# A pre-norm layer with RWKV-7, neighbourhood attention and a mixture of experts on one core: one recurrence direction in reversed time, one block transpose per solve, head-by-head turns, and background matmuls handed out at a fixed rate

## The chip, the cores and the metric

The kernel runs on one core of a Trainium2 chip. The metric is the device time of one execution in microseconds (us), median over runs. Everything is computed in float32 or with pairs of fp32r matmuls that together give float32 accuracy.

## The reference, cut to what matters

One layer. The 256 latent tokens `x` and 256 context tokens `ctx` are modulated, normalised and projected by one large matrix. Two mixers read the projections: RWKV-7, a linear recurrence run in both directions over time, and neighbourhood attention. Their outputs are gated, merged, projected and added to `x`; then 16 experts, two per token, follow.

```python
def rwkv_scan(s0, r, decay, k, v, kk, a, reverse, emit):
    def step(s, inp):
        w_t, k_t, v_t, kk_t, a_t = inp[:5]
        s_kk = jnp.einsum('bhvk,bhk->bhv', s, kk_t)
        s = (s * w_t[:, :, None, :] - s_kk[..., None] * (kk_t * a_t)[:, :, None, :]
             + v_t[..., None] * k_t[:, :, None, :])
        y = jnp.einsum('bhvk,bhk->bhv', s, inp[5]) if emit else None
        return s, y
...
    for d in range(2):
        rev = d == 1
        s_c, yc_d = rwkv_scan(s0, r_c, w_c, kd_c, v_c, kk_c, a_c, rev, emit_ctx)
        _, yx_d = rwkv_scan(s_c, r_x, w_x, kd_x, v_x, kk_x, a_x, rev, True)
        y_x = y_x + yx_d
...
        yb_c, yb_x = na_mixer(z_c, z_x, na_q_g[l], na_k_g[l], na_rpb[l], need_ctx=not last)
        x = x + m_x[2] * branch_merge(z_x[9], z_x[10], ya_x, yb_x, proj_a[l], proj_b[l], w_out[l])
        h2_x = modulate(rms_norm(x, norm2_g[l]), m_x[3], m_x[4])
        x = x + m_x[5] * moe(h2_x, router_w, router_bias, moe_w1[l], moe_w3[l], moe_w2[l])
```

There are 8 heads of 64 channels in the recurrence and two directions, `d = 0` forward and `d = 1` backward.

## The kernel before, in words

The recurrence is cut into chunks of 32 tokens, 8 chunks per stream. It goes first over the context (`s = 0`), then over the latents (`s = 1`), and each of the two passes has three stages that follow one another:

- **prep** (`rw_prep`, L639): decays and keys on VectorE, ScalarE and GpSimd; `products` (L691) multiplies keys by keys within each chunk, on TensorE, one matmul for each chunk and half of the partitions, in blocks of 64 rows by 64 columns with 32 columns of the moving operand; `turn` (L720) transposes the scaled keys `bk` into `BT` (four 128x128 transposes at L727 for each `q`, then four copies of 64x256 out of PSUM at L731).
- **solve** (`rw_solve`, L757): the inverses of all unit triangular 32x32 matrices at once, on VectorE. It transposes the input in 32x32 blocks at L765 (four instructions, one for each 32 partitions; the two of direction 1 write through a reversed-dimension view), runs 31 dependent pairs at L770 and L772, and transposes back at L776 (four instructions). While it runs, `fill()` is called after every second pair.
- **chain** (`rw_chain`, L779): 8 dependent steps, one for each chunk. A step has small matmuls (32x32, 128x32 and 64x64 tiles), an eviction at L801, another at L809, the state update at L822 and, for the latents, the output products.

These three stages are called the recurrence's own work below. The rest of the layer up to the merge, called the other work, is a Python generator `others()` (L1041): values, attention projections and attention for two head groups, receptances, modulation, gates. Its matmuls are 128x128 tiles with 256 or 512 moving columns; every projection is three fp32r products of split operands (`three`, L431). `step()` (L477) advances the generator by at most three matmuls, and `fill()` (L472) at some 160 places of the recurrence's code takes the next number from the hand-written list `FILL` (L160) and makes so many steps. `until(name)` (L1060) steps until a named part is issued. Which instruction then stands where on an engine is decided by the scheduler of the tile layer, with the order of issue as the priority.

A weight unit is split into a high and a low part by ScalarE (L260) and VectorE (L261) when the generator first needs it (`w_unit`, L419). Outputs of 128x256 take one PSUM bank each (`proj_fm` L437, `proj_tm` L450), and each is evicted by its own instruction.

After the recurrence come the output gate, `proj_a`, the merge, the output projection `wo`, the router, and the 16 experts in 8 rounds of two, whose weights come by DMA.

```python
    def fill():
        for _ in range(next(fills, 0)):
            step()
...
        yield from values()
        done.add("v")
        yield from att_proj(0)
        yield from both_(att_core(0), att_proj(1), MIX[0])
        yield from receptances()
```

Of the kernel before, what the change touches and what calls it, by code (L numbers as in the profile page):

```python
# [63 lines left out]
def _constants():  # L64
# [52 lines left out]
def _pack(I):  # L117
# [42 lines left out]
FILL = [  # L160
# [4 lines left out]
]  # L165
ORDER = [(("k0", 1), ("k1", 0))] * 3
MIX = [7, 1]
# [60 lines left out]
def hybrid_kernel(ctx: ExitStack, tc: tile.TileContext, a, out, dbg=None, stop=None):  # L228
# [84 lines left out]
    def turn_x(st, k2):  # L313
        p = pb()
        for k in range(2):
            for i in range(2):
                kc = 2 * k2 + k
                T.transpose(p[:, (2 * k + i) * 128:(2 * k + i + 1) * 128], xn[:, 2 * st + i, kc * 128:(kc + 1) * 128], ident)
        (V.tensor_copy if k2 % 2 else S.copy)(xT[:, 2 * k2:2 * k2 + 2, st * 256:st * 256 + 256], p.rearrange("p (k t) -> p k t", k=2))
# [51 lines left out]
    def w_load():  # L371
        i = n_loaded[0]
        if i < len(SEQ):
# [37 lines left out]
    def w_raw(*name):  # L411
        i = n_used[0]
        n_used[0] += 1
        assert SEQ[i] == name, (SEQ[i], name)
        return wraw[i % NRAW]

    n_split = [0]

    def w_unit(*name):  # L419
# [5 lines left out]
        w_load()  # L425
        v = lambda t: t.r[:, :4 * w].rearrange("p (k c) -> p k c", c=w)
        return v(hi), v(lo)
# [9 lines left out]
    def proj_fm(n, nt):  # L437

        w = GROUPS[n][1]
        res = [pa()[:, :nt] for _ in range(w // 128)]  # L440
        for hf in range(2):
# [4 lines left out]
            yield from three([(res[c], at(wh, k, c), x[k], hf == 0 and k == 0 and x is hs, False) for c, k in ck for x in (hs, us)]  # L446
                             + [(res[c], at(wl, k, c), hs[k], False, hf == 1 and k == 3) for c, k in ck])
        return res

    def proj_tm(n):  # L450

        res = [pa()[:, :256] for _ in range(4)]
        for hf in range(2):
# [3 lines left out]
            yield from three([(res[tt], at(x, tt, k), wh[:, k, :], hf == 0 and k == 0 and x is hh, False) for tt, k in tk for x in (hh, hl)]  # L457
                             + [(res[tt], at(hh, tt, k), wl[:, k, :], False, hf == 1 and k == 3) for tt, k in tk])
        return res
# [9 lines left out]

    fills = iter(FILL)  # L470

    def fill():  # L472

        for _ in range(next(fills, 0)):
            step()

    def step():  # L477
        if filler[0] is not None and next(filler[0], "end") == "end":
            filler[0] = None
# [10 lines left out]
    def first_split(n, q):  # L490
# [8 lines left out]
        if q % 2:  # L499
            w_load()  # L500
# [95 lines left out]
    def mod_gen(m, rows):  # L596
        p = pb()
        for kc in range(8):
            b = w_raw("mod", m, kc)
            mod_part(p, kc, [b[:, 256 * g:256 * g + 256] for g in range(4)])  # L600
            w_load()
# [37 lines left out]
    def rw_prep(s, R):  # L639
# [21 lines left out]
        def decays(f, d):  # L661
# [18 lines left out]
            for h in range(2):  # L680
                r_ = slice(64 * h, 64 * h + 64)
                eng = G if h else V
                eng.tensor_tensor(GG[f][d][r_, h, :, :, 0, :], qc(kk[s][r_, Qs]), E4[r_, :, :, ex], op=ALU.mult)
                if s:
                    eng.tensor_tensor(GG[f][d][r_, h, :, :, 1, :], qc(R["rf"][r_, Qs]), E4[r_, :, :, inc], op=ALU.mult)
            V.scalar_tensor_tensor(bk[:, :, d, :], c16(sg), 0.5, c16(cum), op0=ALU.mult, op1=ALU.mult)
# [33 lines left out]
        def turn(f, d):  # L720
            bk = tmps[d][3]
            for q in range(2):
# [34 lines left out]
    def rw_solve(AT, nA, Xi, tmp):  # L757
# [5 lines left out]
        quarters = [(slice(32 * i, 32 * i + 32), i % 2) for i in range(4)]  # L763
        for ro, d in quarters:
            V.transpose(nA[ro].rearrange("p j s -> p s j") if d else nA[ro], ATg[ro])  # L765
# [9 lines left out]
        for ro, d in quarters:  # L775
            V.transpose(ATg[ro], Xi[ro].rearrange("p j s -> p s j") if d else Xi[ro])  # L776
# [68 lines left out]
    def values():  # L845
        for f in range(2):
            Qs = slice(2 * f, 2 * f + 2)
            for t4, p in enumerate((yield from proj_tm(f"v{f}"))):
                s, tt = divmod(t4, 2)
                S.copy((RC, RX)[s]["vt"][:, :, tt, Qs, :].rearrange("p h q v -> p q h v"), p.rearrange("p (q h v) -> p q h v", h=2, v=64))  # L850
# [13 lines left out]
    def att_proj(g):  # L864
# [6 lines left out]
        qs = yield from proj_fm(f"qB{g}", 256)  # L871
# [5 lines left out]
        for q, p in enumerate(qs):  # L877
            V.tensor_scalar(qB[:, q, :], p, W["qg"], None, op0=ALU.mult)
            S.activation(qsq[:, q, :], p, AF.Square)
        yield  # L880
        vs = yield from proj_tm(f"vB{g}")
        for tt, p in enumerate(vs):
            S.copy(vB[:, tt, :], p)
# [14 lines left out]
    def receptances():  # L898
        RX["rf"] = A.get(4, 256)
        for f in range(2):  # L900
            for q, p in enumerate((yield from proj_fm(f"r{f}", 256))):
                S.copy(RX["rf"][:, 2 * f + q, :], p)
# [8 lines left out]
    def gates_a():  # L911
        ga_alloc()

        (p,) = yield from proj_fm("lg", 256)
# [566 lines left out]
```

## Time and profile before

| what | value |
|---|---|
| median of three runs | 769.55 us (769.16, 769.55, 773.76) |
| the profiled execution's own time | 774.38 us |
| its span, first to last instruction | 772.6 us |
| TensorE (PE) busy, share of the span | 699.7 us, 91% |
| VectorE (DVE) busy | 415.7 us, 54% |
| ScalarE (ACT) busy | 301.4 us, 39% |
| mean granted TensorE clock | 0.919 of full |
| stages by their first own instruction | prep 0 from 72 us, solve 0 from 129, chain 0 from 176, prep 1 from 264, solve 1 from 350, chain 1 from 398, merge and `wo` from 484, experts from 539 |

All times of the rows are us from the start of the span. The time outside the span is 774.38 − 772.6 = 1.8 us.

### The profile page before, as it was taken

Reading aid. Unit: us, or ns where it says so; the run is one execution under the profiler, and the core shown is the slowest. Engines: PE = TensorE matmul, PEld = TensorE weight load, DVE = VectorE, ACT = ScalarE, POOL = GpSimd, SP = SyncE. Lnnn points to the kernel's source line nnn. Section 1 sums busy time; section 2 is a strip of 40 time slices with the busy share of each in tenths; the row PEclk is TensorE's granted clock in tenths of the full one; section 3 lists DMA queues with packets and bytes.
Section 4 is the critical chain, followed back from the end, with each engine's and each line's share of the span. In section 5 each row is a group of like instructions: output and inputs, shape, how many; then the busy total and the mean of one; then the engine's idle time right before and its main releaser. Section 6 shows DMA issues by size and latency. Waiting matters only on the chain. (4 is left out here: it accounts for less than half of the span.)

```text
span 772.6 us, 14457 instructions
## 1 busy us (share of the span) xinstructions
PE 699.7 (91%) x5977; PEld 470.9 (61%) x5977; DVE 415.7 (54%) x750; ACT 301.4 (39%) x604; POOL 101.6 (13%) x90
## 2 busy tenths in 40 slices
PE   4999798998999969888989886998999999999996
PEld 2667576886866735477988663987535435535532
DVE  2537978998654577679985434655122122213112
ACT  5437586526475457545434421432121011101110
POOL 0001533003322061420002311000000000000000
PEclk9999879999978996799989855899999999999999
DMA  9842001412200243677552218687999999999951
GB/s 364 350 151 82 28 28 32 133 57 76 83 29 23 83 164 115 212 251 259 179 189 81 70 57 298 215 299 278 414 389 413 411 410 411 408 408 411 407 237 59
DMA packets 47017, 165.34 MB, mean 214 GB/s; under 512 B 5472, under 2 KB 6880, under 8 KB 46048
## 3 DMA queue, kind: packets, MB, share of 16 engines
q1 hardware_dynamic: 46944, 164.34, 57.4%
q8 instruction: 49, 0.80, 0.4%
q14 instruction: 24, 0.20, 0.1%
HBM read 163.27 MB, written 1.05 MB: 213 GB/s over the span
## 5 line engine op out<-in xcount | busy, mean ns | idle before, releaser
L256 PE MATMUL pa<-arena_p,arena_q 128*128 128x256 f32 (+1 forms) x984 | 165.1, 321 | 6.7 <-ACT arena_q L260 2.3
L256 PE MATMUL pb<-arena 128*32 128x64 f32 (+13 forms) x2248 | 128.8, 291 | 36.1 <-DVE arena L688 9.7
L256 PE MATMUL pa<-arena,arena_m 128*64 128x512 f32 (+1 forms) x692 | 157.6, 563 | 0.0
L256 PEld LDWEIGHTS pa<-arena_p,arena_q 128*128 128x128 f32 x984 | 139.6, 198 | 28.4 <-issue 6.8
L256 PEld LDWEIGHTS pb<-arena 128*32 128x32 f32 (+7 forms) x2246 | 80.9, 150 | 79.8 <-issue 28.8
L256 PEld LDWEIGHTS pa<-arena,arena_m 128*64 128x64 f32 x692 | 51.6, 138 | 90.6 <-issue 86.6
L260 ACT CAST arena_q<-arena 128x1024 fp32r<-128x1024 f32 (+1 forms) x66 | 62.9, 955 | 81.8 <-PE pa L256 59.9
L261 DVE TENSOR_TENSOR arena_q<-arena,arena_q 128x1024 fp32r<-128x1024 f32 (+1 forms) x66 | 76.5, 1160 | 23.9 <-ACT arena_q L260 16.5
L256 PE MATMUL pa<-arena_q,arena_p 128*128 128x256 f32 x384 | 57.6, 299 | 0.0
L1381 DVE TENSOR_TENSOR arena_m<-arena_m,pa 128x512 f32<-128x512 f32 x8 | 5.5, 687 | 95.9 <-PE pa L256 95.9
L256 PEld LDWEIGHTS pa<-arena_q,arena_p 128*128 128x128 f32 x384 | 50.2, 197 | 5.6 <-issue 2.9
L794 POOL TENSOR_TENSOR arena<-arena 64x512 f32<-64x512 f32 x30 | 33.1, 1103 | 145.1 <-DVE arena L822 139.1
L1322 ACT ACTIVATE arena_m<-pa,arena 128x128 f32<-128x128 f32 x32 | 12.1, 458 | 76.3 <-PE pa L256 76.3
L256 PE MATMUL pa<-arena 128*64 128x256 f32 (+5 forms) x192 | 41.4, 488 | 0.3 <-DVE arena L265 0.3
L790 ACT COPY arena<-arena 32x256 f32<-32x256 f32 x64 | 25.8, 403 | 26.7 <-PE pb L256 23.5
L1401 DVE SCALAR_TENSOR_TENSOR arena_m<-pa,arena,arena_p 128x512 f32<-128x512 f32 x16 | 12.0, 751 | 44.8 <-PE pa L256 44.8
L260 ACT CAST arena_r<-arena_m 128x512 fp32r<-128x512 f32 x16 | 9.9, 618 | 66.6 <-DVE arena_m L1401 66.6
L256 PE MATMUL pb<-arena,arena 64*64 64x64 f32 (+1 forms) x496 | 31.2, 278 | 3.5 <-ACT arena L809 2.9
L256 PEld LDWEIGHTS pa<-arena_m,arena_p 128*128 128x128 f32 x256 | 29.2, 192 | 6.6 <-issue 5.7
L256 PE MATMUL pa<-arena_p,arena_m 128*64 128x512 f32 x100 | 32.6, 593 | 0.0
L256 PE MATMUL pa<-arena_m,arena_p 128*128 128x128 f32 x256 | 30.7, 278 | 0.9 <-DVE arena_m L1309 0.9
L256 PEld LDWEIGHTS pb<-arena,arena 64*64 64x64 f32 (+1 forms) x496 | 22.8, 160 | 13.2 <-ACT arena L809 5.2
(208 smaller groups left out, 843.1 us busy)
## 6 DMA issues: line engine op xcount, KB each, us to landing
arena<-in_w_dram SPq DMA_DIRECT2D x142, 512.0 KB, 9.6
arena<-in_win_dram SPq DMA_DIRECT2D x42, 512.0 KB, 3.7
arena<-in_modr_dram SPq DMA_DIRECT2D x32, 512.0 KB, 3.7
arena_p<-in_w_dram SPq DMA_DIRECT2D x25, 512.0 KB, 9.9
arena<-in_modw_dram SPq DMA_DIRECT2D x4, 2048.0 KB, 14.3
arena<-in_w_dram SPq DMA_DIRECT2D x30, 256.0 KB, 8.1
arena_m<-in_w_dram SPq DMA_DIRECT2D x10, 512.0 KB, 8.8
arena<-in_pab_dram SPq DMA_DIRECT2D x8, 512.0 KB, 3.3
```

Of the source, the lines that this page charges most:

```text
L256: return T.matmul(out, lhsT, rhs, start=start, stop=stop, skip_group_check=True)
L260: S.copy(dhi.bitcast(F32R), src)
L261: eng.tensor_tensor(dlo.bitcast(F32R), src, dhi, op=ALU.subtract)
L790: S.copy(Z[rv, h, :, d, :], vt[32 * c4:32 * c4 + 32, h, tt, :, :])
L794: G.tensor_tensor(sd[r_], Z[r_, h], pc[r_, :, :, i].rearrange("p d q -> p q d").unsqueeze(3) .to_broadcast([64, 4, 2, 64]), op=ALU.mult)
L1322: S.activation(dst, src, AF.Identity, scale=m4[:, kc:kc + 1], bias=m3[:, kc:kc + 1])
L1381: V.tensor_tensor(sil.ap, sil.ap, ph[1], op=ALU.mult)
L1401: V.scalar_tensor_tensor(sil.ap, py[n2], gsl[pr % 2].ap, m5r[:, n2 * 512:(n2 + 1) * 512], op0=ALU.mult, op1=ALU.mult)
```

## The change

1. **Direction 1 in reversed time.** The masks and the two writes in `decays` (L683, L688) store direction 1 with time reversed inside each chunk. All 32x32 blocks then have the same triangular form, and the solve transposes all 128 partitions with one instruction at each end.
2. **Turn head by head.** Instead of four 128x128 transposes, 16 matmuls of 64x64 by the identity write straight where `BT` wants them, and one copy of 128x512 takes the place of four of 64x256 (ScalarE for `q = 0`, VectorE for `q = 1`).
3. **Shared PSUM banks.** Two outputs of 128x256 share a bank, so `proj_fm`, `proj_tm` and `wo` take half the banks, and most evictions become 128x512.
4. **Pace.** The list `FILL` goes; `fill()` adds a rate for the stage it stands in (`PACE`, seven stages) and steps when a whole step is due. Each matmul of the other work gets an ordering edge behind the recurrence's own last matmul of three `fill()` calls before (`LAG`), with no semaphore, and a priority 50 places later (`LATER`).
5. **Order of the other work.** `att_proj(1)` comes whole before `att_core(0)`, and the receptances are mixed into `att_core(0)`. Weight units are split one unit ahead, and their loads are driven by which buffers are free. The gates must be issued before the merge (`until("gates")`).

```diff
-        lt = s[None] - j[:, None] if d == 0 else j[:, None] - s[None]
-        c[f"maskG{d}"] = np.concatenate([(lt > 0) * (slot != d)[:, None], lt >= 0], 1)
+        jn, sn = (j, s) if d == 0 else (np.where(slot == 1, 31 - j, j), 31 - s)
+        lt = [(x[None] - jn[:, None]) * (1 - 2 * d) for x in (sn, s)]
+        c[f"maskG{d}"] = np.concatenate([(lt[0] > 0) * (slot != d)[:, None], lt[1] >= 0], 1)
...
-FILL = [
-    11, 0, 2, 0, 2, 0, 2, 2, 2, 0, 2, 2, 0, 5, 5, 4, 2, 0, 3, 0, 2, 1, 2, 2, 2, 0, 2, 4, 4, 0, 0, 1, 0, 0, 2, 2, 0, 2, 2, 2, 2, 2, 2, 2, 2, 2, 2, 2,
...
+PACE = [4.5, 1.62, 2.7, 1.16, 4.0, 2.0, 9.03]
+LAG, LATER = 3, 50
...
+    gates_, own, other = [], [None], [False]
+    ORDERED = mybir.DependencyInfo(mybir.DependencyClass.NoSync, mybir.DependencyReason.DATA)
+
+    def paced(i):
+        if not other[0]:
+            own[0] = i.ins
+        elif len(gates_) > LAG and gates_[-1 - LAG] is not None:
+            tc.add_manual_dep(i.ins, gates_[-1 - LAG].name, ORDERED, reason="pace of the other work")
+        return i
+
     def mm(out, lhsT, rhs, start=True, stop=True):
-        return T.matmul(out, lhsT, rhs, start=start, stop=stop, skip_group_check=True)
+        return paced(T.matmul(out, lhsT, rhs, start=start, stop=stop, skip_group_check=True))
...
-        res = [pa()[:, :256] for _ in range(4)]
+        out_ = [pa() for _ in range(2)]
+        res = [out_[t // 2][:, t % 2 * 256:t % 2 * 256 + 256] for t in range(4)]
...
     def fill():
 
-        for _ in range(next(fills, 0)):
+        gates_.append(own[0])
+        due[0] += PACE[at_stage[0]]
+        while due[0] >= 1:
+            due[0] -= 1
             step()
 
     def step():
-        if filler[0] is not None and next(filler[0], "end") == "end":
-            filler[0] = None
+        if filler[0] is not None:
+            at = tc.cur_priority
+            tc.cur_priority = at + LATER
+            other[0] = True
+            if next(filler[0], "end") == "end":
+                filler[0] = None
+            other[0] = False
+            tc.cur_priority -= LATER
...
-                for i in range(4):
-                    T.transpose(p[:, i * 128:(i + 1) * 128], bk[:, q * 8 + 2 * i:q * 8 + 2 * i + 2].rearrange("p c w t -> p (c w t)"), ident)
-                pv = p.rearrange("p (i h k) -> p i h k", i=4, h=2)
-                for h in range(2):
-                    for c2 in range(2):
-                        (V.tensor_copy if h and c2 else S.copy)(BT[f][64 - 64 * h:128 - 64 * h, d, q, c2:8:2, :],
-                                                                pv[64 * c2:64 * c2 + 64, :, h, :])
+
+                for c in range(8):
+                    for h in range(2):
+                        r_ = slice(64 * h, 64 * h + 64)
+                        mm(p[64 - 64 * h:128 - 64 * h, c * 64:(c + 1) * 64], bk[r_, q * 8 + c].rearrange("p w t -> p (w t)"), ident[r_, r_])
+                (V.tensor_copy if q else S.copy)(BT[f][:, d, q].rearrange("p c k -> p (c k)"), p)
...
-        for ro, d in quarters:
-            V.transpose(nA[ro].rearrange("p j s -> p s j") if d else nA[ro], ATg[ro])
+        V.transpose(nA.ap, ATg)
...
-        for ro, d in quarters:
-            V.transpose(ATg[ro], Xi[ro].rearrange("p j s -> p s j") if d else Xi[ro])
+        V.transpose(ATg, Xi.ap)
...
-        yield from both_(att_core(0), att_proj(1), MIX[0])
-        yield from receptances()
+        yield from att_proj(1)
+        done.add("p")
+        yield from both_(att_core(0), receptances(), MIX[0])
...
+    until("gates")
```

How the order of instructions moves, at three places. In the rows, `pb<-arena 64x32` (or `64x64`, `64x128`) are the recurrence's own matmuls and `pa<-arena_q,arena_p` or `pa<-arena_p,arena_q` are those of the other work; xN is N in a row.

TensorE in prep 0, the products of the first half, before:

```order
L256 MATMUL pb<-arena 64x32 x8
L256 MATMUL pa<-arena_q,arena_p 128x256 x6
L727 MATMUL pb<-arena 128x128 x8
L256 MATMUL pa<-arena_q,arena_p 128x256 x9
L727 MATMUL pb<-arena 128x128 x8
L256 MATMUL pa<-arena_q,arena_p 128x256 x9
L256 MATMUL pb<-arena 64x32 x8
```

The same place in the changed kernel, with buffer numbers:

```order
L266 MATMUL pa_652<-arena_q_69,arena_p_65 128x256 x3
L266 MATMUL pb_782<-arena_61 64x32
L266 MATMUL pa_652<-arena_q_69,arena_p_65 128x256
L266 MATMUL pb_782<-arena_61 64x32
L266 MATMUL pa_652<-arena_q_69,arena_p_65 128x256
L266 MATMUL pb_783<-arena_61 64x32
L266 MATMUL pa_652<-arena_q_69,arena_p_65 128x256
L266 MATMUL pb_783<-arena_61 64x32
```

Before, own and other matmuls stood in groups of 6 to 16; now single ones alternate. The same holds for the turns, which are now `pb<-arena 64x64` and alternate one by one with `pa<-arena_p,arena_q 128x512`. Counted over prep 0, the other work's unbroken runs of matmuls go from 16 (162 matmuls) to 157 (431 matmuls), 130 of them of one matmul.

TensorE at the last two steps of chain 1, before:

```order
L256 MATMUL pb<-arena,arena_73 64x64
L256 MATMUL pb<-arena 64x32
L256 MATMUL pb<-arena,arena_73 64x64 x15
L256 MATMUL pb<-arena 64x32 x15
L256 MATMUL pb<-arena 32x64 x32
L256 MATMUL pb<-arena 64x32 x16
```

The same place in the changed kernel:

```order
L266 MATMUL pb<-arena,arena_73 64x64 x15
L266 MATMUL pb<-arena 64x32 x15
L266 MATMUL pa<-arena_p,arena_q 128x256 x3
L266 MATMUL pb<-arena 32x64 x2
L266 MATMUL pa<-arena_p,arena_q 128x256 x5
L266 MATMUL pb<-arena 32x64 x14
L266 MATMUL pa<-arena_p,arena_q 128x256 x11
L266 MATMUL pb<-arena 32x64 x16
L266 MATMUL pa<-arena_p,arena_q 128x256 x4
```

The last steps of chain 1 had no other work between their matmuls; now every step has about 25 to 36 of its matmuls there, in five or six runs. Over chain 1 the runs go from 20 to 51.

VectorE at the start of solve 0, before (L711 masks the products, L731 evicts the turn):

```order
L711 TENSOR_TENSOR arena<-pb,arena 64x8x32 x4
L765 STREAM_TRANSPOSE arena<-arena 32x1024 x2
L711 TENSOR_TENSOR arena<-pb,arena 64x8x32 x4
L765 STREAM_TRANSPOSE arena<-arena 32x32x32
L731 COPY arena_73<-pb 64x4x64 x2
L765 STREAM_TRANSPOSE arena<-arena 32x32x32
```

The same place in the changed kernel (L755 masks the products, L274 splits weights, the others belong to the other work):

```order
L755 TENSOR_TENSOR arena<-pb,arena 64x8x32 x4
L806 STREAM_TRANSPOSE arena<-arena 128x1024
L274 TENSOR_TENSOR arena_q<-arena,arena_q 128x1024
L278 TENSOR_SCALAR arena<-pa 128x8
L280 RECIPROCAL arena<-arena 128x8
```

The four transposes are one, behind the last mask, and the four transposes at the end of a solve become one in the same way. Counted over the whole program on TensorE, the other work's matmuls that stand ahead of prep 1's start are 840 before (129 with the first projections, 162 in prep 0, 116 in solve 0, 358 in chain 0, 75 between) and 832 now (96, 431, 74, 223, 8).

## Rows read from the trace of the kernel before

**Rows 1.** The page: busy time by engine, and the chain that ended last.

```profile
PE 699.7 (91%) x5977; PEld 470.9 (61%) x5977; DVE 415.7 (54%) x750; ACT 301.4 (39%) x604; POOL 101.6 (13%) x90
...
PE 40%; DVE 3%; ACT 1%; DMA 1%; issue 0%; POOL 0%; DVEq 0%; ACTq 0%; POOLq 0%
```

**Rows 2.** Windows by stage: stretch, length, busy by engine, clock, DMA share, GB/s.

```profile
72.00:129.00 57.00, 47.13 (x504) 38.55 (x503) 45.66 (x57) 40.69 (x81) 24.46 (x18) 0.85 0.12 37
129.00:176.00 47.00, 46.37 (x315) 37.47 (x313) 44.08 (x89) 19.62 (x36) 2.96 (x3) 1.00 0.26 79
176.00:258.00 82.00, 79.12 (x1026) 57.25 (x1027) 51.94 (x93) 49.84 (x103) 22.06 (x19) 0.90 0.19 56
...
264.00:350.00 86.00, 72.27 (x658) 44.35 (x655) 63.57 (x98) 50.90 (x110) 30.36 (x24) 0.82 0.54 183
...
466.00:484.00 18.00, 10.72 (x31) 5.00 (x31) 9.79 (x18) 4.20 (x6) 2.93 (x3) 0.59 0.76 286
...
539.00:763.00 224.00, 222.85 (x1203) 102.46 (x1204) 49.99 (x117) 33.23 (x76) 0.00 (x0) 0.99 0.95 376
```

**Rows 3.** Timeline, TensorE, prep 0: start, length, instructions, count (an own matmul has two records).

```profile
113.30 0.97 PE L256 MATMUL pa<-arena_q,arena_p 128*128 128x256 f32 x6
114.20 0.43 PE L256 MATMUL pb<-arena 64*64 64x32 f32 x16
114.57 0.97 PE L256 MATMUL pa<-arena_q,arena_p 128*128 128x256 f32 x6
...
123.59 0.43 PE L256 MATMUL pb<-arena 64*64 64x32 f32 x16
```

**Rows 4.** Timeline, TensorE, between chain 0 and prep 1.

```profile
257.08 6.86 PE L256 MATMUL pa<-arena_p,arena_q 128*128 128x256 f32 x55
263.87 1.70 PE L256 MATMUL pb<-arena 128*32 128x256 f32 x10
```

**Rows 5.** Timeline, TensorE, short runs in chain 0 and chain 1.

```profile
195.04 0.39 PE L256 MATMUL pa<-arena_q,arena_p 128*128 128x256 f32 x1
195.36 0.68 PE L256 MATMUL pb<-arena,arena 64*64 64x64 f32 x16
...
409.49 0.68 PE L256 MATMUL pb<-arena 32*32 32x64 f32 x32
410.10 0.73 PE L256 MATMUL pa<-arena_p,arena_q 128*128 128x256 f32 x4
410.76 0.32 PE L256 MATMUL pb<-arena,arena 64*64 64x64 f32 x2
411.02 0.30 PE L256 MATMUL pb<-arena 128*64 128x32 f32 x2
411.25 0.63 PE L256 MATMUL pa<-arena_p,arena_q 128*128 128x256 f32 x3
```

**Rows 6.** Timeline, VectorE, the block transposes of solve 0.

```profile
121.53 2.50 DVE L765 STREAM_TRANSPOSE arena<-arena 32x1024 f32<-32x1024 f32 x2
...
129.84 1.97 DVE L765 STREAM_TRANSPOSE arena<-arena 32x1024 f32<-32x1024 f32 x1
...
170.45 6.53 DVE L776 STREAM_TRANSPOSE arena<-arena 32x1024 f32<-32x1024 f32 x4
```

**Rows 7.** Windows between state updates (L822) of chain 1, TensorE's `pa` tiles alone.

```profile
405.30:415.70 10.40, 6.21 (x39) 1.00 0.24 71
...
426.20:434.70 8.50, 2.73 (x14) 1.00 0.24 83
434.70:441.40 6.70, 0.00 (x0) 0.80 0.23 75
441.40:449.20 7.80, 0.00 (x0) 0.50 0.01 2
```

**Rows 8.** Groups by line: the turn's evictions, and 128x512 copies.

```profile
L731 ACT COPY arena<-pb 64x256 f32<-64x256 f32 x48 | 17.6, 366 | 2.4 <-PE pb L727 1.7
L946 ACT COPY arena<-pa 128x512 f32<-128x512 f32 x16 | 9.1, 579 | 3.7 <-PE pa L945 3.6
```

More of the change, by code (lines that the diff above doesn't have):

```diff
@@ L369, in w_source, with w_load @@
         return a["win"][:, o:o + 4 * w], w
-    def w_load():
-        i = n_loaded[0]
-        if i < len(SEQ):
+    free = set(range(-NRAW, 0))
+    def w_load(done=None):
+        if done:
+            free.add(AT[done])
+        while n_loaded[0] < len(SEQ) and n_loaded[0] - NRAW in free:
+            i = n_loaded[0]
             n_loaded[0] += 1
@@ L411, in w_raw, with w_parts @@
     def w_raw(*name):
-        i = n_used[0]
-        n_used[0] += 1
-        assert SEQ[i] == name, (SEQ[i], name)
+        i = AT[name]
+        assert i < n_loaded[0], name
         return wraw[i % NRAW]
-    n_split = [0]
-    def w_unit(*name):
+    AT = {n: i for i, n in enumerate(SEQ)}
+    n_split, ready = [0], {}
+    def w_parts(*name):
         raw = w_raw(*name)
@@ L424, in w_unit @@
         n_split[0] += 1
-        w_load()
+        w_load(name)
         v = lambda t: t.r[:, :4 * w].rearrange("p (k c) -> p k c", c=w)
-        return v(hi), v(lo)
+        ready[name] = v(hi), v(lo)
+    def w_unit(*name):
+        if name not in ready:
+            w_parts(*name)
+        nxt = next((n for n in SEQ[AT[name] + 1:] if n[0] != "mod"), None)
+        if nxt and AT[nxt] < n_loaded[0]:
+            w_parts(*nxt)
+        return ready.pop(name)
     def three(products):
@@ L439, in proj_fm @@
         w = GROUPS[n][1]
-        res = [pa()[:, :nt] for _ in range(w // 128)]
+        if nt == 512:
+            res = out_ = [pa() for _ in range(w // 128)]
+        else:
+            out_ = pa()[:, :2 * w]
+            res = [out_[:, c * 256:(c + 1) * 256] for c in range(w // 128)]
         for hf in range(2):
@@ L456, in proj_tm @@
             tk = [(tt, k) for tt in range(4) for k in range(4)]
-            yield from three([(res[tt], at(x, tt, k), wh[:, k, :], hf == 0 and k == 0 and x is hh, False) for tt, k in tk for x in (hh, hl)]
+            yield from three([(res[tt], at(x, tt, k), wh[:, k, :], hf == 0 and k == 0 and x is hh and tt % 2 == 0, False) for tt, k in tk for x in (hh, hl)]
                              + [(res[tt], at(hh, tt, k), wl[:, k, :], False, hf == 1 and k == 3) for tt, k in tk])
-        return res
+        return out_
     def run(g):
@@ L847, in values @@
             Qs = slice(2 * f, 2 * f + 2)
-            for t4, p in enumerate((yield from proj_tm(f"v{f}"))):
-                s, tt = divmod(t4, 2)
-                S.copy((RC, RX)[s]["vt"][:, :, tt, Qs, :].rearrange("p h q v -> p q h v"), p.rearrange("p (q h v) -> p q h v", h=2, v=64))
+            for s, p2 in enumerate((yield from proj_tm(f"v{f}"))):
+                for tt in range(2):
+                    S.copy((RC, RX)[s]["vt"][:, :, tt, Qs, :].rearrange("p h q v -> p q h v"),
+                           p2[:, tt * 256:tt * 256 + 256].rearrange("p (q h v) -> p q h v", h=2, v=64))
         for q2 in range(2):
@@ L870, in att_proj @@
             S.activation(ksq[:, q, :], p, AF.Square)
-        qs = yield from proj_fm(f"qB{g}", 256)
+        pq_ = yield from proj_fm(f"qB{g}", 256)
         p = pa()
@@ L900, in receptances @@
         for f in range(2):
-            for q, p in enumerate((yield from proj_fm(f"r{f}", 256))):
-                S.copy(RX["rf"][:, 2 * f + q, :], p)
+            S.copy(RX["rf"][:, 2 * f:2 * f + 2, :].rearrange("p q t -> p (q t)"), (yield from proj_fm(f"r{f}", 256)))
     lg = A.get(256)
@@ L912, in gates_a @@
         ga_alloc()
-        (p,) = yield from proj_fm("lg", 256)
+        p = yield from proj_fm("lg", 256)
         S.activation(lg.ap, p, AF.Tanh, scale=0.5)
@@ L918, in gates_a @@
         for i in range(4):
-            for c, p in enumerate((yield from proj_fm(f"gA{i}", 256))):
-                S.activation(gA[i][:, c * 256:(c + 1) * 256], p, AF.Tanh, scale=0.5)
+            S.activation(gA[i].ap, (yield from proj_fm(f"gA{i}", 256)), AF.Tanh, scale=0.5)
     P.put(hh.parts(2)[0])
@@ L1209, in hybrid_kernel @@
     for n4 in range(4):
-        pp = [pa()[:, :256] for _ in range(2)]
+        pw = pa()
+        pp = [pw[:, c * 256:(c + 1) * 256] for c in range(2)]
         for hf in range(2):
@@ L1216, in hybrid_kernel @@
                     ws, ls = wh[:, k, c * 128:(c + 1) * 128], wl[:, k, c * 128:(c + 1) * 128]
-                    mm(o, ws, mgh.r[:, kc, :], start=kc == 0, stop=False)
+                    mm(o, ws, mgh.r[:, kc, :], start=kc == 0 and c == 0, stop=False)
                     mm(o, ws, mgl.r[:, kc, :], start=False, stop=False)
@@ L1362, in late_rows @@
         p = pa()
-        T.transpose(p[0:1, 0:128], over[:, 0:1], ident)
+        turn128(p[0:1, 0:128], over[:, 0:1], ident)
         V.tensor_reduce(over[0:1, 0:1], p[0:1, 0:128], axis=AX.X, op=ALU.max)
```

57 lines of the change are left out of this document (32 added, 25 removed), and 3 rows, old and new, of the table FILL.

## The prediction

> **What bounds the kernel now.** I read the page's busy shares and chain first, then the busy times by stage, then TensorE's timeline inside the stages. TensorE is busy 91% of the span and the chain that ended last runs over it for 40% of the span and over no other engine for more than 3% [rows 1]. By stages [rows 2] the picture differs. From 72 to 258 us TensorE is busy 47.1 of 57, 46.4 of 47 and 79.1 of 82 us, and the 6.8 us up to prep 1 are one unbroken run of other work [rows 4]: 179.4 of 192 us in all. So this stretch ends when TensorE has done its share of own and other work, while VectorE has to keep up in the solve (44.1 of 47). Prep 1 has 14 us of idle TensorE, chain 1 is a chain of dependent steps (below), and the experts, from 539 us, are bound by TensorE (222.9 of 224 us), not touched by the change; they shift as a whole. So the sum is about 72 to 484 us.
>
> "Busy" hides something there. Fifty-five other-work matmuls of 128x256 in a row start 6.79 us (257.08 to 263.87) before what follows, 0.123 each [rows 4]. One alone holds the next instruction off by 0.32 us (195.04 to 195.36), four by 0.66 (410.10 to 410.76), six by 0.90 (113.30 to 114.20): about 0.17 to 0.20 plus 0.123 for each [rows 3, 5]. The own small tiles do the same: 16 matmuls (32 records) take 0.61, 8 take 0.37, one takes 0.26 or 0.23, so some 0.2 plus 0.02 to 0.03 each [rows 3, 5]. No waiting engine is named in these rows. Each change between a full-size and a small tile therefore costs about 0.2 us, and a single own matmul followed by a single one of the other work takes 0.54 to 0.58 us where 0.15 would do inside runs. I take 0.39 us for each extra round trip, the lower end.
>
> The Trainium skill has a rule for this: "TensorEngine Tiling (Array Packing)", section Key Properties, says that changing the tiling mode, and not only the tile, drains TensorE. By that rule the price falls on every round trip; the rows above agree with it, but the trace of before has no long stretch of single alternation that would show it at this density.
>
> **The change part by part.**
>
> *Pace and order.* The work itself hardly changes: 840 matmuls of the other work stood ahead of prep 1, now 832, which is −8 × 0.123 = −1 us. What changes is how finely it is mixed. In prep 0 its runs go from 16 to 157, an extra 141 round trips × 0.39 = +55 us of TensorE time. In solve 0, chain 0 and behind it the runs fall by 7 in all, in prep 1 and solve 1 they rise by 7; I leave these out. TensorE takes its instructions in program order, so own matmuls wait in line: before, the last own product of prep 0 was issued at 123.59 us [rows 3] and the solve could start; now 269 more matmuls and the 55 us stand mostly ahead of it. TensorE was idle 12.6 us of the stretch before, 9.9 of them in prep 0 [rows 2]; with so much work moved forward it won't wait in prep 0: I give 10 us back (bounds 0 and 13). The bounds of the 55 are 0 (were the gaps no price of the change of tile) and 141 × 0.43 = 61.
>
> *Transposes of the solve.* Four instructions at the start end at 131.8 us, the last of them 1.97 us long, and the four at the end take 6.53 us in one piece, with the chain behind them [rows 6]. One plain instruction over 32 partitions takes 2.50 / 2 = 1.25 us; no row shows one over 128 partitions. Its bounds are 1.25 (partitions side by side) and 6.5 (four quarters in turn); I take 1.25, the nearest shape with the same 1024 elements for each partition. That saves 6.53 − 1.25 = 5.3 and 0.7 at solve 0, and 5.3 and about 2.7 (two reversed ones of 1.97 less one plain) at solve 1: −6 and −8 us, counted in full because the chain's first state update needs the solved blocks. If quarters ran in turn: 0 and 0.
>
> *Turn.* Three of four evictions lie on ScalarE, 48 × 0.366 = 17.6 us; eight copies of 128x512 at 0.579 replace them, 4.6 us [rows 8]. I count these 13 us at nothing, since ScalarE is busy only 40.7 of 57 us in prep 0 and TensorE is now the slower one; without that cover up to −6 us would come from each prep. The 16 small matmuls are own ones and are in the count of runs.
>
> *Shared banks, split ahead.* Fewer evictions and earlier splits take work from ScalarE and VectorE, which TensorE hardly waits for between 72 and 258 us. Zero, bounds −4 to 0; a bank now waits for two outputs, which costs up to 2.
>
> *Prep 1.* 38 fewer of the other work's matmuls, −4.7 us of TensorE, of which half counts, since prep 1 had 14 us of idle TensorE [rows 2]: −2.
>
> *Chain 1.* Between two state updates the time was 10.4 us with 39 of the other work's matmuls, 8.5 with 14, and 6.7 to 7.8 with none, at a clock of 0.80 and 0.50 [rows 7]. The changed kernel has about 25 in every step, so by the rows 8.5 + 11 × (10.4 − 8.5) / 25 = 9.3. Six such intervals took 51.8 us and will take 56; with a first step that has 58 matmuls more and a last one that is no longer empty I take +9 us, bounds +3 and +14. Behind it the merge has nothing less to wait for; its clock of 0.59 [rows 2] may rise, up to −3 us; I take none.
>
> *Sum.* Prep 0 to the start of prep 1: +55 − 1 − 6 − 10 = +38. Prep 1 −2, solve 1 −8, chain 1 +9. Total +37 us. The profiled execution, 774.4 us, would become 811; the median of the runs stands 4.8 us below that, so the forecast is 769.55 + 37 = 806.5 us.
>
> **The rivals.**
>
> *The price of alternation isn't there, and the kernel gets faster.* The mechanism: in the single alternation of prep 0 the next weights are loaded behind the running matmul and the 0.2 us vanish. For it: the rows of before show the gap mostly at the ends of longer runs. Against it: the same gap stands behind runs of 1, 4, 6 and 16. Then the sum is 0 − 1 − 6 − 10 = −17, −2, −8, and 0 in chain 1: −27, 743 us. The sum is linear between the two cases, so the sign turns at 0.39 × 27 / 64 = 0.16 us a round trip; below that the change pays.
>
> *Half the price.* One of the two changes of a round trip is hidden, 0.195 us: +27 − 1 − 6 − 10 = +10, −10, and +3 in chain 1: 773 us, no difference that can be told.
>
> *The clock falls in the alternating stretch.* In prep 0 the granted clock was 0.85 on the mean, and where chain 1 ran its small matmuls alone it was 0.50, the lower of the two levels [rows 2, 7]. Those bare steps are short groups of small tiles with waits between; single alternation is nearer to them than to unbroken runs. If a third of the some 150 us in prep 0 is granted the lower level, the other work's part of it (some 86 us of dense time, of which a third doubles) adds 86 / 3 = 28 us: 834 us. Against it: in solve 0 and chain 0, with other work beside own, it was 1.00 and 0.90.
>
> The Trainium skill warns in "TensorE: Matmul & The Clock Gate", section "A second HAM failure mode: psum-queue depth-cycling", of a kernel in which short idle times between groups of matmuls made the clock go up and down; the granted clock of 0.50 in the bare steps of chain 1 agrees, and no run here shows it for alternation.
>
> **How the numbers follow.** The forecast has a chance of 0.51, the clock 0.18, no price 0.15, half price 0.16. What a measurement of this kernel tells from no change is about 1%, 7.7 us, so 762 to 777 is "the same". Faster: no price and a little of half price, 0.17. The same: most of half price, 0.12. Slower: 0.71. The range must take in half price and the clock and leaves out only the case without a price: 763 to 842 us. The forecast's own range, by the bounds of its terms (price 0.33 to 0.43, slack 0 to 13, chain 1 +3 to +14), is 790 to 825.
>
> **What would show it right or wrong.** Right: the timeline of prep 0 has rows of x1 and x2 that start about 0.3 and 0.25 us apart; solve 0's recursion starts at 168 to 202 us and not 132 (55 − 10 later, and up to 33 more by the 269 moved matmuls at 0.123), prep 1 starts near 302 and not 264; the 128x1024 transposes take about 1.25 us; the steps of chain 1 take some 9.3 us, all with other work; the experts take 224 us as before. The forecast is wrong if the alternating rows stand less than 0.16 us apart on the mean over dense work, if a 128-partition transpose takes several us, or if prep 0 is done before 140 us with the other work spread over it.

## The result: 853.5 us, slower by a tenth, and the profile after

The changed kernel takes 853.50 us (median of four runs, 840.93 to 854.72) beside 769.36 before: a ratio of 1.100, 95% interval 1.084 to 1.116. The forecast had the direction and the place, and less than half of the size: +37 us were forecast, +84 came, and the result lies outside the range. The spread of the four runs goes with the granted clock: the run of 840.93 has a mean of 0.923, the others 0.908 to 0.910.

The profiled execution spans 852.3 us, 79.7 more than before. Milestones of the two traces divide the spans into seven stretches and say where the loss lies:

| from ... to | before | after | difference |
|---|---|---|---|
| start to chain 0's first state update | 185.8 | 297.7 | +111.9 |
| to chain 0's last state update | 72.2 | 68.5 | −3.7 |
| to the last mask of prep 1 | 88.9 | 69.5 | −19.4 |
| to chain 1's first state update | 58.4 | 53.1 | −5.3 |
| to chain 1's last state update | 52.6 | 51.7 | −0.9 |
| to the first matmul of the experts | 81.4 | 78.5 | −2.9 |
| experts | 233.3 | 233.3 | 0.0 |

So the loss is one stretch, the one that holds prep 0 and solve 0, and it is larger than the whole difference. The page and the windows of the changed kernel (same columns as in [rows 1, 2]; the last number but two is the clock):

```profile
PE 799.1 (94%) x6425; PEld 521.0 (61%) x6425; DVE 392.5 (46%) x728; ACT 282.4 (33%) x544; POOL 100.4 (12%) x90
```

```profile
72.00:298.00 226.00, 216.16 (x1257) 151.85 (x1257) 90.52 (x147) 62.38 (x105) 28.13 (x23) 0.75 0.12 37
...
138.00:168.00 30.00, 30.00 (x156) 17.02 (x156) 6.31 (x8) 4.87 (x7) 2.87 (x4) 1.00 0.06 18
168.00:224.00 56.00, 56.00 (x352) 41.85 (x351) 17.40 (x24) 13.45 (x19) 3.87 (x2) 0.75 0.16 48
224.00:268.00 44.00, 44.00 (x132) 23.76 (x131) 13.33 (x35) 2.68 (x3) 1.00 (x1) 0.50 0.06 17
...
489.00:541.00 52.00, 51.57 (x965) 44.25 (x962) 28.61 (x45) 25.32 (x54) 12.65 (x12) 1.00 0.28 91
```

TensorE gained 99 us of busy time although the work is almost the same. The profile shows it without idle time from 138 to 268 us, while VectorE is busy 37 and ScalarE 21 of these 130 us, and the clock is 0.75 on the mean over the stretch to chain 0, which of the two levels means the lower one for half of it. Between 224 and 268 us it is at the lower level throughout while TensorE has 44.0 of 44 us busy. The timeline shows what it does there. Prep 0, the products (a pair is one matmul of the other work, x1, and one own matmul, x2 records):

```profile
104.66 0.38 PE L266 MATMUL pa<-arena_q,arena_p 128*128 128x256 f32 x1
104.97 0.30 PE L266 MATMUL pb<-arena 64*64 64x32 f32 x2
105.20 0.39 PE L266 MATMUL pa<-arena_q,arena_p 128*128 128x256 f32 x1
...
109.51 0.58 PE L266 MATMUL pa<-arena_q,arena_p 128*128 128x256 f32 x1
110.02 0.42 PE L266 MATMUL pb<-arena 64*64 64x32 f32 x2
110.37 0.58 PE L266 MATMUL pa<-arena_q,arena_p 128*128 128x256 f32 x1
...
115.53 2.71 PE L266 MATMUL pa<-arena_q,arena_p 128*128 128x256 f32 x11
```

The turns, at the full and at the lower clock:

```profile
140.43 0.49 PE L266 MATMUL pa<-arena_p,arena_q 128*128 128x512 f32 x1
140.86 0.33 PE L266 MATMUL pb<-arena 64*64 64x64 f32 x2
141.11 0.49 PE L266 MATMUL pa<-arena_p,arena_q 128*128 128x512 f32 x1
...
224.34 0.79 PE L266 MATMUL pa<-arena_p,arena_q 128*128 128x512 f32 x1
225.07 0.47 PE L266 MATMUL pb<-arena 64*64 64x64 f32 x2
225.47 0.79 PE L266 MATMUL pa<-arena_p,arena_q 128*128 128x512 f32 x1
```

At the full clock a pair takes 105.20 − 104.66 = 0.54 us, the price read from [rows 3, 5]. At the lower level the same pair takes 110.37 − 109.51 = 0.86, and the pair with 512 columns 1.13 in place of 0.68. A group of eleven at the lower level fills 2.7 us, where twelve at the full one take 1.6 (E1 below). The low clock is paid by every matmul that runs at it, alternating or not.

### The profile page after: what moved, and what is told of

Its sections match the earlier page's. It is cut to its first block, busy times and chain, and to the rows that moved or that the text cites. A ratio compares the mean times of both kernels' runs of the same rounds, so it can differ in the third digit from the quotient of the medians.

```text
span 852.3 us, 15245 instructions
## 1 busy us (share of the span) xinstructions
PE 799.1 (94%) x6425; PEld 521.0 (61%) x6425; DVE 392.5 (46%) x728; ACT 282.4 (33%) x544; POOL 100.4 (12%) x90
## 4 chain that ended last, share of the span: by engine, by line
PE 47%; DVE 4%; ACT 2%; DMA 2%; issue 0%; POOL 0%; DVEq 0%; ACTq 0%; POOLq 0%
PE pa L266 35%; PE pb L266 10%; PE pa L269 1%; DMA arena<-in_modr_dram 1%; DVE arena_q L274 1%; DMA arena<-in_win_dram 1%; PE pb L269 0%; DVE arena L1194 0%; ACT arena_q L273 0%; ACT arena L702 0%; DVE arena_m L1457 0%; DVE arena L280 0%; DVE arena L813 0%; DVE arena L729 0%; DVE arena L727 0%
## 5 line engine op out<-in xcount | busy, mean ns | idle before, releaser
L266 PE MATMUL pb<-arena 64*64 64x64 f32 (+10 forms) x2760 | 197.8, 271 | 27.0 <-DVE arena L841 8.8
L266 PE MATMUL pa<-arena_p,arena_q 128*128 128x256 f32 (+1 forms) x984 | 212.6, 347 | 3.9 <-ACT arena_p L366 1.2
L266 PEld LDWEIGHTS pb<-arena 64*64 64x64 f32 (+5 forms) x2758 | 121.6, 141 | 117.2 <-issue 64.3
L266 PEld LDWEIGHTS pa<-arena_p,arena_q 128*128 128x128 f32 x984 | 147.8, 201 | 30.9 <-issue 3.5
L266 PE MATMUL pa<-arena,arena_m 128*64 128x512 f32 (+1 forms) x692 | 154.3, 557 | 0.0
L274 DVE TENSOR_TENSOR arena_q<-arena,arena_q 128x1024 fp32r<-128x1024 f32 (+1 forms) x66 | 74.6, 1130 | 73.0 <-PE pa L266 28.9
L266 PE MATMUL pa<-arena_q,arena_p 128*128 128x256 f32 x384 | 78.9, 344 | 0.0
L266 PEld LDWEIGHTS pa<-arena_q,arena_p 128*128 128x128 f32 x384 | 61.3, 227 | 7.7 <-issue 2.3
L266 PE MATMUL pa<-arena_p,arena_m 128*64 128x512 f32 x100 | 36.2, 594 | 0.0
L266 PE MATMUL pb<-arena,arena 64*64 64x64 f32 (+1 forms) x496 | 27.9, 261 | 1.3 <-ACT arena L849 1.0
L755 DVE TENSOR_TENSOR arena<-pb,arena 64x256 f32<-64x256 f32 (+1 forms) x32 | 17.7, 552 | 24.9 <-PE pb L266 22.3
```

The source lines that it names most:

```text
L266: return paced(T.matmul(out, lhsT, rhs, start=start, stop=stop, skip_group_check=True))
L274: eng.tensor_tensor(dlo.bitcast(F32R), src, dhi, op=ALU.subtract)
L755: V.tensor_tensor(Gd[ro:ro + 64, h].rearrange("p q c w t -> p (q c) (w t)")[:, par::2], pv[o_:o_ + 64], mG[o_:o_ + 64, 0:w].unsqueeze(1).t ...
```

## The experiments

Two theories. *Grain*: the cost is the number of changes between full-size and small tiles on TensorE, each at its price, and with many of them the clock goes to the lower level. *Amount*: 269 more matmuls stand ahead of solve 0, and that costs however they are mixed. Runs of the other work are counted in the order of the built programs, over prep 0 and its turns; "before" was timed beside each set, at 765 to 768 us.

**E1, the same amounts in groups.** With edges and no offset of the priority the scheduler puts the other work's matmuls back into groups.

```diff
-LAG, LATER = 3, 50
+LAG, LATER = 3, 0
```

> The changed kernel with LATER = 0 in place of 50. On TensorE nearly as much other work stands in each stage as in the changed kernel (prep 0 with its turns 431 matmuls, as before this edit), but in groups: in prep 0 its runs fall from 157 to 28, single ones from 130 to 0; in chain 1 from 51 to 41. Theory grain (each extra round trip between full-size and small tiles costs 0.43 us at the full clock and 0.63 at the half, as the changed kernel's rows show): 129 round trips fewer are 55 to 81 us, so 772 to 798 us. Theory amount (269 more matmuls ahead of the solve and the solve's recursion behind them are the cost, however they are mixed): within 15 us of the changed kernel, 838 to 855 us.

Measured: 761.88 us, ratio to before 0.998 (0.993 to 1.004). The edit takes 92 us off the changed kernel and leaves 431 matmuls in prep 0 as they were. Against the kernel before, grain is the loss and amount isn't. The bracket for grain, 55 to 81 us, was missed by 10 us. The timeline of E1 has groups of 12 and 15 where the changed kernel alternates, and the clock over its stretch up to chain 0's first update is 0.92 in place of 0.75:

```profile
136.91 1.69 PE L266 MATMUL pa<-arena_q,arena_p 128*128 128x256 f32 x12
138.53 0.43 PE L266 MATMUL pb<-arena 64*64 64x32 f32 x16
138.89 2.05 PE L266 MATMUL pa<-arena_q,arena_p 128*128 128x256 f32 x15
```

```profile
72.00:201.00 129.00, 114.37 (x1231) 97.54 (x1231) 93.64 (x146) 60.24 (x102) 27.58 (x23) 0.92 0.20 64
```

**E2, everything but the pace.** `PACE`, edges and `LATER` out, the list `FILL` back.

```diff
-PACE = [4.5, 1.62, 2.7, 1.16, 4.0, 2.0, 9.03]
-LAG, LATER = 3, 50
+FILL = [
...
+LAG, LATER = 10**6, 0
...
-        gates_.append(own[0])
-        due[0] += PACE[at_stage[0]]
-        while due[0] >= 1:
-            due[0] -= 1
-            step()
+        for _ in range(next(fills, 0)):
+            step()
```

> The changed kernel with the list FILL of before in place of PACE, without ordering edges and without LATER: reversed time, one transpose, turn head by head, shared banks, splits one unit ahead and the new order of the other work stay. In prep 0 the runs are 16, as before. If the pace is the whole loss: 745 to 765 us, since the transposes alone give 6 to 14 us. If one of the other parts costs (a turn of 16 small matmuls, a bank that two outputs wait for): 780 us or more.

Measured: 749.78 us, ratio 0.983 (0.978 to 0.989). The other parts together are a gain of 13 to 16 us (by the ratio and by the medians); the pace alone made the change a loss. Of the pace's three parts it is the offset `LATER`: E1 keeps the rates and the edges without it and is as fast as before, E9 below keeps it without the edges and is nearly as slow as the changed kernel.

**E3, the grain alone, in the kernel before.** The other work's matmuls in the products of prep 0 are queued and issued one after each own matmul.

```diff
         for i, m in enumerate(products):
-            mm(*m)
+            queue.append(m)
             if i % 3 == 2 or i == len(products) - 1:
+                if not drops[0]:
+                    flush()
                 yield
...
                            Gd[r_, h, j // 8, j % 8].rearrange("p w t -> p (w t)"))
+                        if drops[0]:
+                            drip()
```

> The kernel before, in whose prep 0 the other work's matmuls that fall into a group of products are issued one by one between the own ones, as many as before: runs in prep 0 from 18 to 51, 39 of them single; every other stage the same. Theory grain: 33 round trips more at 0.43 to 0.63 us are 14 to 21 us, less up to 10 us in which TensorE was idle in prep 0: 773 to 790 us. Theory amount: no change, 765 to 773 us.

Measured: 786.51 us, ratio 1.033 (1.025 to 1.042): +21 us by the medians and 25 by the ratio for 33 round trips, 0.64 to 0.77 each. The amounts are those of before, so this is the grain by itself, with what it does to the clock. Its windows show where the clock fell, and the timeline the same pair of 0.86 us as in the changed kernel:

```profile
96.00:117.00 21.00, 20.11 (x177) 16.64 (x176) 17.71 (x27) 17.55 (x37) 10.17 (x9) 0.73 0.08 27
117.00:148.00 31.00, 31.00 (x141) 21.86 (x142) 6.46 (x11) 5.68 (x10) 3.87 (x2) 0.51 0.05 17
```

```profile
118.56 0.58 PE L256 MATMUL pa<-arena_q,arena_p 128*128 128x256 f32 x1
119.06 0.42 PE L256 MATMUL pb<-arena 64*64 64x32 f32 x2
119.42 0.58 PE L256 MATMUL pa<-arena_q,arena_p 128*128 128x256 f32 x1
```

**E4, reversed time alone.** The four lines of the masks, `go` in the two writes of `decays`, and one transpose at each end of the solve, put into the kernel before.

```diff
-        for ro, d in quarters:
-            V.transpose(nA[ro].rearrange("p j s -> p s j") if d else nA[ro], ATg[ro])
+        V.transpose(nA.ap, ATg)
```

> The kernel before with the reversed time of direction 1 and one block transpose at each end of a solve, and nothing else. By the prediction's term, 6 us at solve 0 and 8 at solve 1: 755 to 760 us. If TensorE's other work sets the end of the solve anyway: 765 to 771 us.

Measured: 752.54 us, ratio 0.984 (0.976 to 0.992), −13 us; −14 were forecast, though the interval allows −6 to −18. The time is 2 us under the expected band. The instruction over 128 partitions takes what one over 32 takes [rows 6]:

```profile
L774 DVE STREAM_TRANSPOSE arena<-arena 128x1024 f32<-128x1024 f32 x2 | 2.5, 1240 | 0.0
```

**E5 and E6, how the price grows with the count.** `LATER` is 50 in a part of prep 0 alone: in the turns (E5), or up to them (E6).

```diff
-LAG, LATER = 3, 50
+LAG, LATER = 3, [0]
...
             bk = tmps[d][3]
+            LATER[0] = 0 if s else 50
...
+            LATER[0] = 0
```

> The changed kernel in which LATER is 50 only for the steps made inside turn() of prep 0 and 0 everywhere else. Runs of the other work in prep 0 and its turns: 48 (22 single), against 28 (none single) with LATER = 0 everywhere and 157 (130 single) with 50; the amounts in each stage are those of LATER = 0. If each round trip costs the same, 92 us for 129 of them is 0.71 us: 20 of them are 14 us, so 776 us. If only their density counts (the clock falls only where the alternation is long): 762 to 768 us.

> The changed kernel in which LATER is 50 up to the turns of prep 0 and 0 inside them and behind prep 0. Runs in prep 0 and its turns: 131 (103 single). At 0.71 us a round trip, 103 more than with LATER = 0: 73 us, so 835 us. If the alternation in the turns (128x512 matmuls) costs much more than that in the products: below 810 us. Chain 1 has 41 runs in place of 51; if these 10 cost as well, up to 7 us less than that.

Measured: E5 769.71 us, E6 833.98 us. Against E1 that is 7.8 us for 20 round trips, 0.39 each, and 72 us for 103, 0.70 each; the changed kernel has 92 us for 129, 0.71 each. E5 lies between its two expectations, 762 to 768 and 776; by the spread of its runs and of E1's its price is 0.27 to 0.63 a round trip. The windows up to chain 0's first update show a difference in the clock: E5 keeps it at 0.92, as E1, and E6 goes down to 0.81. E5 first, then E6:

```profile
72.00:209.00 137.00, 122.41 (x1237) 100.19 (x1235) 93.99 (x146) 60.51 (x102) 28.58 (x23) 0.92 0.19 60
```

```profile
72.00:273.00 201.00, 190.42 (x1252) 140.25 (x1251) 90.06 (x145) 61.92 (x104) 28.14 (x23) 0.81 0.13 41
```

So a round trip costs some 0.4 us where the clock holds, and 0.7 on the mean where it falls. That it falls because the alternation is long is not shown: E3 lost the full clock with 33 more round trips, and the changed kernel kept it through 27 us of alternation, from 138 to 165 us. E5's pairs have 512 columns, those of E3 and most of E6's have 256; number and kind were not varied apart. E5's alternation, from 125 to 134 us, runs at the full clock, with pairs of 0.68 us:

```profile
125.56 0.49 PE L266 MATMUL pa<-arena_p,arena_q 128*128 128x512 f32 x1
125.99 0.33 PE L266 MATMUL pb<-arena 64*64 64x64 f32 x2
126.24 0.49 PE L266 MATMUL pa<-arena_p,arena_q 128*128 128x512 f32 x1
```

**E7 and E8, the turn and the order.** E2 with the old turn, and E2 with the old order of the other work and the old proportion of its mixing. E7 undoes the lines of part 2 of the change; the lines below are E8's, beside those of E2.

```diff
-MIX = [2, 1]
+MIX = [7, 1]
...
-        yield from att_proj(1)
-        done.add("p")
-        yield from both_(att_core(0), receptances(), MIX[0])
+        yield from both_(att_core(0), att_proj(1), MIX[0])
+        yield from receptances()
```

> The kernel with the old list (the changed kernel without PACE, edges and LATER) and the turn of before: four 128x128 transposes and four evictions of 64x256 for each q. Theory that the turn is worth little (its evictions lie on ScalarE and beside TensorE's work): 747 to 753 us, as with the new turn. Theory that the chain behind it waits for the evictions: 3 to 6 us slower than the new turn, 753 to 756 us.

> The kernel with the old list and also the order of the other work of before: the second group's projections mixed into the first group's attention, receptances alone. The list was written for that order. If the order matters for the list: 740 to 746 us. If it doesn't: 747 to 753 us.

Measured: 750.19 and 748.73 us, ratios 0.978 and 0.976 (0.969 to 0.985 and 0.983): both the same as E2 within what can be told. The turn's 13 us of ScalarE time were rightly counted at nothing, and the order of the other work shows no effect.

**E9, no edges.**

```diff
-LAG, LATER = 3, 50
+LAG, LATER = 10**6, 50
```

> The changed kernel with LAG so large that no matmul gets an ordering edge. The order on TensorE has the same 158 runs of the other work in prep 0 and its turns, 132 of them single, and moves 30 matmuls into chain 0 from the stages around it. If the edges themselves cost time on the engines: 835 us or less. If only where the matmuls stand counts: 840 to 858 us, as with the edges.

Measured: 838.3 us (two runs), ratio 1.095 (1.085 to 1.105). The edges themselves aren't the loss: without them the matmuls alternate as before this edit, and the time is 2 us under the expected band and under the changed kernel's own lowest run. The clock of its stretch is 0.84 in place of 0.75: in the alternation with 512 columns it came back at 232.6 us, behind a run of five matmuls of the other work, while the changed kernel stayed at the lower level behind the same run up to 268 us. E9:

```profile
219.00:232.60 13.60, 13.60 (x47) 6.99 (x45) 5.99 (x21) 0.00 (x0) 0.00 (x0) 0.50 0.02 8
232.60:250.00 17.40, 17.40 (x79) 9.46 (x78) 6.35 (x14) 1.63 (x2) 0.00 (x0) 1.00 0.09 30
```

By the pairs, 35 us more at the lower level cost 35 × (1 − 0.68 / 1.13) = 14 us, an estimate that is nearly the whole difference to the changed kernel's median. The changed kernel's run of 840.93 us has the mean clock of E9's runs, 0.923 beside 0.921 and 0.922, so the difference need not come from the edges. Why the clock came back in one and not in the other is open.

**E10, the solve's recursion.** In the changed kernel the recursion of solve 0 takes 66.5 us from its first pair (224.2) to its last, before 37.6, because instructions in VectorE's queue wait for TensorE in its midst. VectorE's waits in that stretch of the changed kernel (us in total, times, longest):

```profile
DVE arena L775 <- PE pb L266: 17.6, 2, 11.6
DVE arena_q L274 <- PE pa L266: 12.5, 2, 11.1
```

```diff
-                (V.tensor_copy if q else S.copy)(BT[f][:, d, q].rearrange("p c k -> p (c k)"), p)
+                S.copy(BT[f][:, d, q].rearrange("p c k -> p (c k)"), p)
```

> The changed kernel with all copies of the turn on ScalarE; in the changed kernel two of VectorE's copies stand inside the recursion of solve 0 and wait for TensorE. The runs on TensorE are those of the changed kernel up to chain 0. Theory that TensorE's order sets the end of this stretch: the recursion of solve 0 (66.5 us from its first pair to its last) gets shorter, but chain 0's first state update stays within 4 us of the changed kernel's 297.7, and the time within 840 to 856 us. Theory that the stalled recursion is a loss of its own: chain 0 starts 6 us or more earlier, and the time falls as much.

Measured: 851.78 us (two runs), chain 0's first update at 293.9. The time is that of the first theory, but its mechanism is only half right: the recursion hardly got shorter (221.9 to 287.2, 65.2 us). With the copies gone the next split of weights waits instead, longer:

```profile
246.27 1.22 DVE L274 TENSOR_TENSOR arena_q<-arena,arena_q 128x1024 fp32r<-128x1024 f32 x1 [16.73 <-PE pa L266]
```

So VectorE's instructions of the recursion stand behind one that waits for TensorE, whichever it is; that the stalled recursion is no loss of its own is not shown by this run, since it stayed stalled.

**E11, groups and a lower rate in prep 0.** What remains between E1 (762) and E2 (750)?

```diff
-PACE = [4.5, 1.62, 2.7, 1.16, 4.0, 2.0, 9.03]
-LAG, LATER = 3, 50
+PACE = [2.0, 3.0, 4.4, 1.5, 3.0, 2.4, 9.03]
+LAG, LATER = 3, 0
```

> LATER = 0 as in the first experiment, and PACE 2.0, 3.0, 4.4, 1.5, 3.0, 2.4, 9.03 in place of 4.5, 1.62, 2.7, 1.16, 4.0, 2.0, 9.03: 189 matmuls of the other work in prep 0 and its turns in place of 431, 164 in solve 0 in place of 89, 289 in chain 0 in place of 192; runs nearly the same (25 in prep 0 and its turns, 37 in chain 0, 39 in chain 1). If work moved ahead of the solve costs, beside its grain: 745 to 755 us, as with the old list. If it doesn't: 757 to 765 us, as with LATER = 0 alone.

Measured: 749.80 us, ratio 0.979 (0.972 to 0.986). The rates of E1 cost some 12 us beside the grain: chain 0's first update comes at 175.0 in place of E1's 200.5 us, and half of these 25 us is given back in prep 1, which then holds more of the other work (84.6 in place of 72.9 us). A rate by stage does as well as the hand-written list once the matmuls stay in groups. By their medians E2, E4, E7, E8 and E11 are 13 to 18 us faster than before; they can't be told apart from each other.

## Why the prediction had the side and not the size

- **The step that failed** is the first term, "an extra 141 round trips × 0.39 = +55 us": it prices every round trip at the full clock, and the sum puts the lower clock at nothing. The count was right, and so was the pair, 0.54 us. E5's 0.39 a round trip at the full clock agrees, though its bounds are so wide that the equal digits are luck. What the runs showed in its place is 0.70 to 0.71 us a round trip where the clock falls (E6, the changed kernel), 92 us by E1. The pairs allow an estimate of how it divides. By their mean clocks the changed kernel's stretch has 113 us at the lower level (half of 226) and E1's 21; the 92 us more lose 92 × (1 − 0.54 / 0.86) = 34 us. E1's stretch is 97 us shorter, so 63 are left, 0.49 a round trip. I had the clock as a rival, with 0.18, as something beside the price and for a third of the stretch; it came together with the price.
- **The rivals.** "The price isn't there" and "half the price" fall with the pairs of 0.54 us and with E3. "The clock falls" happened, and was undersized at 834 us: it had a third of 150 us at the lower level, and charged the other work's dense time alone (86 us, which the prediction doesn't work out; 431 × 0.123 would be 53, and more by those with 512 columns), while own matmuls and the changes between tiles get longer as well (0.86 in place of 0.54 us). By the rule of the Trainium skill named in the prediction ("TensorEngine Tiling (Array Packing)", Key Properties: a change of tiling mode drains TensorE) every round trip should pay, and the trace agrees with 0.54 us for each pair at the full clock. Whether what is paid is a drain or something else in the change, such as the load of the next weights, no run here tells.
- **The credit of 10 us** for idle TensorE failed too. Without the alternation the terms of the sum give −18 us (−1 − 6 − 10 − 2 − 8 and +9); E1 measured −4. The idle time (13.4 us by [rows 2], not 12.6, since the run of 6.8 us begins before 258) was not filled, it moved: the stretch to chain 0's first update has 12.4 us of it before, 9.8 in the changed kernel and 14.6 in E1, 7.0 of these in solve 0, which has less of the other work left. E11, with less work moved forward, measured −18, but is another schedule than the forecast's. Before, then E1:

```profile
72.00:186.00 114.00, 101.62 (x908) 82.67 (x906) 98.55 (x160) 67.29 (x130) 28.48 (x22) 0.91 0.19 56
...
155.00:194.00 39.00, 32.04 (x332) 27.42 (x330) 36.98 (x81) 11.53 (x17) 2.57 (x3) 0.96 0.25 79
```

- **Solve 0.** The forecast let the recursion start at 168 to 202 us; it started at 224 and then lasted 29 us longer, since VectorE waited for TensorE inside it (30 us by the waits above). The forecast had costed the wait before the solve, not the one within it. Its 168 to 202 also adds its 45 and 33 us to the last own product at 123.6, not to the start at 132 that it names; from there they give 177 to 210.
- **Transposes**: right, 1.24 us over 128 partitions, and −13 us (E4) for −14.
- **Turn, banks, splits, order**: right at about nothing. E2 is 3 us under E4, less than the intervals; banks and splits were not tried alone.
- **Chain 1**: +9 forecast, −0.9 measured. The step of 9.3 us failed: with 23 to 28 matmuls of the other work the steps took 7.7 to 8.6 us at a clock of 1.00, and 8.5 on the mean of all six. The first two, which had 39 and 38 before, got shorter by 2.5 and 2.8 us; the last three, which had none and a clock of 0.80 and 0.50 before [rows 7], longer by 1.3 to 1.7 us; the two cancel. The changed kernel's first and last step, TensorE's `pa` tiles alone:

```profile
488.80:496.70 7.90, 4.17 (x24) 1.00 0.35 125
...
530.60:539.80 9.20, 5.98 (x37) 1.00 0.50 169
```

- **Prep 1**: −2 forecast, −19.4 measured. The 6.8 us run ahead of it [rows 4] is gone, and its clock was 0.93 (line below) where before it was 0.82 [rows 2]. The stretch is 72.9 us long in E1 too, and 88.4 in E2 with the old list, beside 88.9 before, so most of the gain goes with the rates; it was not tried alone.

```profile
390.00:442.00 52.00, 51.69 (x657) 32.31 (x655) 37.22 (x65) 33.22 (x67) 19.10 (x16) 0.93 0.60 204
```

## What to carry to other kernels

When two streams of matmuls with different tile shapes share TensorE, count in the issue order how often the shape changes, and price each change from start-to-start times, not from busy time, which hides it. Before a forecast multiplies that price, ask what the granted clock does in such a stretch: in three runs here it fell, and a round trip then cost 0.6 to 0.8 us on the mean in place of some 0.4. Pacing background work by a rate did as well here as the hand-written list once it came in groups (E11); look at the built order, since a change of a priority can turn groups into single alternation without any line of the work changing.

## What the runs showed of the hardware that was not expected

TensorE ran at the lower clock while the profile shows it busy without a gap: 44.0 of 44 us at 0.50 (224 to 268 us). So the busy share alone does not tell the clock; the granted clock has to be read beside it.

The Trainium skill tells in "TensorE: Matmul & The Clock Gate", section "A second HAM failure mode: psum-queue depth-cycling", of short idle times between groups that make the clock go up and down. The rows agree in the going up and down (0.75 on the mean, 0.51 in E3), but have no idle time on record for it between 138 and 268 us; since the ends of matmuls are modelled in the profile, very short ones can't be ruled out.

What TensorE did around these changes can be read from the lengths of its matmuls. In the changed kernel's stretch each of seven returns to the full clock (at 97, 121, 138, 179, 196, 217 and 268 us) stands in an unbroken run of 6 to 57 matmuls of the other work or within 1 us behind it. Five of the falls (at 107, 125, 169, 189 and 206 us) stand in or just behind single alternation with 256 columns. The fall at 169 and the return at 179 us:

```profile
168.57 0.38 PE L266 MATMUL pa<-arena_p,arena_q 128*128 128x256 f32 x1
168.89 0.47 PE L266 MATMUL pb<-arena 64*64 64x64 f32 x2
169.29 0.58 PE L266 MATMUL pa<-arena_p,arena_q 128*128 128x256 f32 x1
...
174.78 3.57 PE L266 MATMUL pa<-arena_p,arena_q 128*128 128x256 f32 x15
178.28 0.43 PE L266 MATMUL pb<-arena 64*64 64x32 f32 x6
178.64 0.58 PE L266 MATMUL pa<-arena_p,arena_q 128*128 128x256 f32 x1
179.15 0.30 PE L266 MATMUL pb<-arena 64*64 64x32 f32 x4
179.38 0.38 PE L266 MATMUL pa<-arena_p,arena_q 128*128 128x256 f32 x1
```

The alternation with 512 columns ran at the full clock from 138 to 165 us and in E5, and at the lower one from 224 to 265 us; what decides was not found.

The lower level doesn't double a pair: 0.54 to 0.86 us, and 0.68 to 1.13.
